# Layer 1's v in two chunks of 1024 columns, all of it by the seven products, with banks of 512 and the token operands from a transposed difference of rows

## The chip, the core and the metric
The kernel runs on one core of a Trainium2 chip. The metric is the device time of one launch in microseconds (us), lower is better. The engines are TensorE (PE, matmuls; PEld are its weight loads), VectorE (DVE), ScalarE (ACT), GpSimdE (POOL) and SyncE (SP), which issues the transfers. Each works through a queue of its own in the order in which the program was scheduled, and waits for semaphores of the others.

## The reference, cut to what matters
Two layers act on 1024 tokens of 1024 channels. Layer 0 is gated recurrence beside windowed attention with one output projection. Layer 1 is a gated MLP whose input projection has three parts of 2048 columns:

```python
h = rms_norm(x, norm_c[j])
z = h @ w_in_c[j]                       # 1024 x 1024 by 1024 x 6144
u, v, g = split_cols(z, (GMLP_WIDTH, GMLP_WIDTH, GMLP_WIDTH))
v = layer_norm(v, ln_v_g[j], ln_v_b[j])
sg = chunked_spatial_gating(v, spatial_w[j], spatial_b[j])
y = u * sg * jax.nn.silu(g)
x = x + y @ w_out_c[j]
```
This case is about v = h @ w_in_c[:, 2048:4096] and the statistics of its layer norm.

## The kernel before
Every float32 operand of a matmul is split into a high and a low part (`hi` by a cast on ACT, `lo` by a subtract on DVE), and `mm3` (lines 145 to 148) multiplies by three matmuls: high by high, high by low, low by high. Larger products are done by Winograd's form of the 2 x 2 block product, seven block products instead of eight, which needs sums and differences of the blocks of both factors. `winograd` (line 739) does so for layer 0's output projection in 14 steps `s`; each step has 48 matmuls of 512 columns, and `operands(s + 1)` is prepared during step s. Its hook `out_a_after` (line 1027) starts layer 1's work: row norms as the token tiles (128 tokens each) come out, and the transposes of tiles 0 to 3 (`norm_c_transpose`) in steps 12 and 13.

Tokens fall into two halves and channels (the contraction) into two halves, so h has the blocks b11, b21 (tokens 0 to 511, channel halves 0 and 1), b12, b22 (tokens 512 to 1023). The token operands t1 = b12 - b11, t2 = b22 - t1, t3 = b22 - b12 and t4 = b21 - t2 serve v, the gate g and u. v is made in two ways:
- columns 0 to 511 (`v_tile`, line 987): plainly, eight token tiles by eight channel blocks, 192 matmuls of 512 columns, with weights from the list of prefetched weights (`weight("v", j)`). Behind each of the first four token tiles PE transposes one of the tiles 4 to 7, and ACT and DVE make its token operands out of the transposed banks (`token_sums`, line 1063); `token_sum_last` makes t4 during tiles 4 to 7.
- columns 512 to 2047 in three chunks of 512 (`v_chunk`, line 1136): seven products, each of 4 token tiles by 4 channel blocks by three matmuls of 256 columns, two tiles sharing a bank. `v_operands` makes the weight operands: `make(i)` one of the seven, its sums where needed, then a cast on ACT and a subtract on DVE.

Results go through `vst` tiles to `vdram`, statistics of 256 columns (`bn_stats`) into `st_all`; behind v the statistics are aggregated and the groups of g and u follow (`group_operands`, `group_gate`), whose first raw weights use the two `raw` buffers.

Order: PE keeps the program's order throughout. The block from `v_tile(0)` to the end of the groups is a `manual_schedule` of ACT, DVE, POOL and SP too: each keeps the program's order inside it, as inside winograd's block ahead of it; where two blocks meet, the scheduler may let the head of the second run ahead of the tail of the first. Buffers: `wpool` has five high and five low weight tiles, `rawpool` two tiles, `big` 16 tiles of 8 KB a partition, PSUM eight banks. The pool `vp` (40 KB a partition) lies where winograd's pool `po` lay, and a tile of it waits until the tiles that lay there were last used.

Of the kernel before, what the change touches and what calls it, by code (L numbers as in the profile page):

```python
# [62 lines left out]
def trunk_kernel(  # L63
# [52 lines left out]
    for j in range(4):  # L116
        add_spec(("v", j), cols_k2(w_in_c, 256 * j, GW))

    wtiles, raws = [], {}
    ahead, last_spec = [0], [index["v", 0] - 1]  # L120

    def fetch_weights(i):

        for j in range(len(raws), min(i, last_spec[0]) + 1):
            raws[j] = rawpool.tile([P, specs[j].shape[1], specs[j].shape[2]], F32, tag="raw", name=f"raw{j}")
            nc.sync.dma_start(out=raws[j], in_=specs[j])

    def load_weights(i, prefetch=True):

        for j in range(len(wtiles), min(i, last_spec[0]) + 1):  # L130
# [850 lines left out]
    st_all = const_c.tile([P, NT, 8, 6], F32, name="st_all")  # L981

    def v_stats(t, g, src):
        for i in range(2):
            nc.vector.bn_stats(out=st_all[:, t, g + i, :], in_=src[:, i * 256:(i + 1) * 256])

    def v_tile(t):
        acc = bank(f"v0_{t}")
        for k in range(8):
            wh, wl = weight("v", k // 2)  # L990
            mm3(acc, h_at(h1h, k, t * P, P), h_at(h1l, k, t * P, P), wh[:, k % 2, :], wl[:, k % 2, :],
                k == 0, k == 7)
# [9 lines left out]
    def norm_c_transpose(t):  # L1002
        for hs, part in ((h1h, "h"), (h1l, "l")):
            for i in range(2):
                if hs[i][t // 4] is None:
                    hs[i][t // 4] = big_tile(F32R, f"g{part}{i}{t // 4}").rearrange("p (k s) -> p k s", k=4)
        return list(norm_transpose(x1_row(t), f"c{t}", h1h, h1l, t))
# [18 lines left out]

    def out_a_after(s, j, m):
# [17 lines left out]
    last_spec[0] = len(specs) - 1  # L1045
    p4.close()
    p5 = ExitStack()
    late["vp"] = p5.enter_context(tc.tile_pool(name="vp", bufs=1, reuse_waits="tile"))


    tsum = [[None] * 2 for _ in range(4)]
    t2_tiles = [late["vp"].tile([P, 2, 4, P], F32, tag=f"vsum{i}", name=f"t2w{i}") for i in range(2)]
    t2_whole = [t2_tiles[i // 2][:, i % 2] for i in range(4)]

    def token_split(i, c, src):
# [3 lines left out]
        hi, lo = [part[:, :, c * P:(c + 1) * P] for part in tsum[i]]  # L1059
        nc.scalar.copy(out=hi, in_=src)  # L1060
        nc.vector.tensor_tensor(out=lo, in0=src, in1=hi.bitcast(F32), op=ALU.subtract)

    def token_sums(c, banks):

        b12, b22 = banks
        b11h, b11l = [part[0][0][:, :, c * P:(c + 1) * P].bitcast(F32) for part in (h1h, h1l)]
        t1, t3 = [late["vp"].tile([P, 4, P], F32, tag="sum", name=f"t{i}w{c}", bufs=4) for i in (1, 3)]
        t2 = t2_whole[c]
        nc.scalar.copy(out=t3, in_=b12)
        nc.vector.tensor_tensor(out=t1, in0=b12, in1=b11h, op=ALU.subtract)  # L1070
        nc.vector.tensor_tensor(out=t1, in0=t1, in1=b11l, op=ALU.subtract)
        nc.vector.tensor_tensor(out=t2, in0=b22, in1=t1, op=ALU.subtract)
        token_split(0, c, t1)
        nc.vector.tensor_tensor(out=t3, in0=b22, in1=t3, op=ALU.subtract)
        token_split(1, c, t2)
        token_split(2, c, t3)

    def token_sum_last(c):

        b21h, b21l = [part[1][0][:, :, c * P:(c + 1) * P].bitcast(F32) for part in (h1h, h1l)]  # L1080
        t2 = t2_whole[c]
        nc.vector.tensor_tensor(out=t2, in0=b21h, in1=t2, op=ALU.subtract)
        nc.vector.tensor_tensor(out=t2, in0=t2, in1=b21l, op=ALU.add)
        token_split(3, c, t2)

    def v_operands(vc):

        raw = []
        for d in range(2):
            for kh in range(2):  # L1090
                pool, tag = (late["vp"], f"raw{kh}") if d else (rawpool, "raw")
                raw.append(pool.tile([P, 4, 256], F32, tag=tag, name=f"rawv{vc}_{d}{kh}"))
                nc.sync.dma_start(out=raw[-1], in_=cols_k4(w_in_c, kh, GW + vc * 512 + d * 256))
        a11, a12, a21, a22 = raw
        sums, ops = [], []

        def make(i):
            if i == 2:
                sums.extend(late["vp"].tile([P, 4, 256], F32, tag=f"vsum{j}", name=f"vs{vc}_{j}") for j in range(2))
                nc.vector.tensor_tensor(out=sums[0], in0=a21, in1=a22, op=ALU.add)  # L1100
                nc.vector.tensor_tensor(out=sums[1], in0=sums[0], in1=a11, op=ALU.subtract)
            elif i == 4:
                nc.vector.tensor_tensor(out=a11, in0=a11, in1=a21, op=ALU.subtract)
            elif i == 5:
                nc.vector.tensor_tensor(out=a12, in0=a12, in1=sums[1], op=ALU.subtract)
            src = [a11, a12, *sums[::-1], a11, a12, a22][i] if i > 1 else raw[i]
            hi = wpool.tile([P, 4, 256], F32R, tag="wh", name=f"whv{vc}_{i}")
            lo = wpool.tile([P, 4, 256], F32R, tag="wl", name=f"wlv{vc}_{i}")
            nc.scalar.copy(out=hi, in_=src)
            nc.vector.tensor_tensor(out=lo, in0=src, in1=hi.bitcast(F32), op=ALU.subtract)  # L1110
            ops.append((hi, lo))

        return ops, make

    manual = tc.manual_schedule(engines={ET.Activation, ET.DVE, ET.Pool, ET.SP})
    manual.__enter__()
    for t in range(4):
        v_tile(t)
        token_sums(t, norm_c_transpose(4 + t))
    for t in range(4, NT):  # L1120
        v_tile(t)
        if t == 4:
            ops, make = v_operands(1)
            make(0)
        token_sum_last(t - 4)
    b11, b21, b22 = [(h1h[i][j], h1l[i][j]) for i, j in ((0, 0), (1, 0), (1, 1))]
    bops = {"b11": b11, "b21": b21, "b22": b22, "t1": tsum[0], "t2": tsum[1], "t3": tsum[2], "t4": tsum[3]}

    plan = [(0, False, "b11"), (1, False, "b21"), (0, True, "t2"), (2, False, "t1"), (0, True, "t3"), (2, True, "b22"),
            (0, True, "t4")]  # L1130
# [317 lines left out]
```

## Time and profile before

| | us |
|---|---|
| median of 3 runs | 1338.87 (1338.86 to 1339.13) |
| profiled execution | 1339.43 |
| its span, first to last instruction | 1337.7 |
| mean granted TensorE clock in it | 0.998 of 2.4 GHz |

The profile is of one execution, and durations are taken from it. 1.73 us of its time lie outside the span. A page gives the busy share of each engine; the trace behind it is asked by views: groups of instructions by line, the timeline of one engine, busy time by stretches, waits, the chain that ended last, transfers. Matmuls are pipelined, so the time of one is longer than its distance to the next; the distance from start to start is what PE pays.

### The profile page before, as it was taken

Reading aid. Unit: us, or ns where it says so; the run is one execution under the profiler, and the core shown is the slowest. Engines: PE = TensorE matmul, PEld = TensorE weight load, DVE = VectorE, ACT = ScalarE, POOL = GpSimd, SP = SyncE. Lnnn points to the kernel's source line nnn. Section 1 sums busy time; section 2 is a strip of 40 time slices with the busy share of each in tenths; the row PEclk is TensorE's granted clock in tenths of the full one; section 3 lists DMA queues with packets and bytes.
Section 4 is the critical chain, followed back from the end, with each engine's and each line's share of the span. In section 5 each row is a group of like instructions: output and inputs, shape, how many; then the busy total and the mean of one; then the engine's idle time right before and its main releaser. Section 6 shows DMA issues by size and latency. Waiting matters only on the chain.

```text
span 1337.7 us, 17905 instructions
## 1 busy us (share of the span) xinstructions
PE 1312.3 (98%) x6775; PEld 1119.6 (84%) x6775; DVE 968.0 (72%) x1594; ACT 690.9 (52%) x1246; POOL 236.3 (18%) x240
## 2 busy tenths in 40 slices
PE   7999999999999999999998999999999999999998
PEld 6988888888878888788887999888888888888887
DVE  6568787877678988987896655585666656579873
ACT  6467777786497776344553223334434444433431
POOL 3345555655323322000000000000000000000000
PEclk9999999999999999999999999999999999999999
DMA  6011111111311106413312332413333233596131
GB/s 226 23 58 49 32 49 32 48 49 32 87 40 56 36 5 231 162 48 142 111 53 90 126 111 80 156 57 111 103 112 110 70 110 103 195 376 231 48 110 63
DMA packets 97170, 131.38 MB, mean 98 GB/s; under 512 B 4907, under 2 KB 68540, under 8 KB 95036
## 3 DMA queue, kind: packets, MB, share of 16 engines
q1 hardware_dynamic: 97084, 130.24, 28.9%
q8 instruction: 53, 0.87, 0.3%
q14 instruction: 33, 0.27, 0.1%
HBM read 105.03 MB, written 25.19 MB: 97 GB/s over the span
## 4 chain that ended last, share of the span: by engine, by line
PE 72%; DVE 13%; ACT 7%; DMA 4%; issue 3%; SPq 0%; POOL 0%; DVEq 0%; ACTq 0%
PE m L146 6%; PE m L148 6%; PE m L147 6%; PE u L147 4%; PE u L148 4%; PE u L146 4%; PE g L146 4%; PE g L147 4%; PE g L148 4%; PE v L146 3%; PE v L147 3%; PE v L148 3%; PE s L1329 2%; PE pq L146 2%; PE pq L148 2%
## 5 line engine op out<-in xcount | busy, mean ns | idle before, releaser
L146 PE MATMUL m<-wh_w,wa 128*128 128x512 f32 x432 | 168.6, 390 | 1.6 <-DVE x L853 1.6
L148 PE MATMUL m<-wh_w,wa 128*128 128x512 f32 x432 | 168.1, 389 | 0.0
L147 PE MATMUL m<-wl_w,wa 128*128 128x512 f32 x432 | 168.1, 389 | 0.0
L146 PEld LDWEIGHTS m<-wh_w,wa 128*128 128x128 f32 x432 | 81.1, 188 | 19.2 <-ACT wa L718 1.8
L148 PEld LDWEIGHTS m<-wh_w,wa 128*128 128x128 f32 x432 | 81.1, 188 | 16.9
L147 PEld LDWEIGHTS m<-wl_w,wa 128*128 128x128 f32 x432 | 81.1, 188 | 16.6
L725 ACT CAST wh_w<-b 128x1024 fp32r<-128x1024 f32 x36 | 37.7, 1047 | 75.4 <-DVE b L820 54.2
L550 DVE CUSTOM_DVE_ANT_0 e<-ps,e,sink_bc 128x256 f32<-128x256 f32 (+1 forms) x128 | 62.0, 520 | 3.1 <-POOL e L525 2.6
L135 DVE TENSOR_TENSOR wl<-raw,wh 128x1024 fp32r<-128x1024 f32 x38 | 50.6, 1337 | 16.4 <-ACT wh L134 16.3
L566 ACT ACTIVATE e<-e,nm 128x256 f32<-128x256 f32 (+1 forms) x128 | 61.4, 481 | 0.0
L853 DVE TENSOR_TENSOR x<-m,x 128x512 f32<-128x512 f32 x56 | 36.6, 685 | 29.5 <-PE m L148 29.5
L1301 ACT ACTIVATE sg<-sg 128x512 f32<-128x512 f32 x24 | 15.2, 632 | 70.4 <-DVE sg L1300 70.4
L574 POOL TENSOR_TENSOR e<-e 128x512 f32<-128x512 f32 x28 | 37.2, 1327 | 80.2 <-ACT e L566 80.2
L146 PE MATMUL pq<-hh,wh 128*128 128x512 f32 x128 | 50.4, 394 | 0.0
L146 PE MATMUL ga<-hh,wh 128*128 128x512 f32 x128 | 50.1, 392 | 0.3 <-ACT z L873 0.3
L146 PE MATMUL gb<-hh,wh 128*128 128x512 f32 x128 | 50.1, 391 | 0.0
L148 PE MATMUL pq<-hh,wl 128*128 128x512 f32 x128 | 50.0, 390 | 0.0
L147 PE MATMUL pq<-hl,wh 128*128 128x512 f32 x128 | 50.0, 390 | 0.0
L148 PE MATMUL gb<-hh,wl 128*128 128x512 f32 x128 | 49.9, 390 | 0.0
L148 PE MATMUL ga<-hh,wl 128*128 128x512 f32 x128 | 49.9, 390 | 0.0
L147 PE MATMUL gb<-hl,wh 128*128 128x512 f32 x128 | 49.9, 390 | 0.0
L147 PE MATMUL ga<-hl,wh 128*128 128x512 f32 x128 | 49.9, 390 | 0.0
(401 smaller groups left out, 4039.2 us busy)
## 6 DMA issues: line engine op xcount, KB each, us to landing
raw<-in_w_in_a_dram SPq DMA_DIRECT2D x34, 512.0 KB, 4.0
b<-in_w_out_a_dram SPq DMA_DIRECT2D x22, 512.0 KB, 3.4
b<-in_w_out_c_dram SPq DMA_DIRECT2D x22, 512.0 KB, 6.0
rawg<-in_w_in_c_dram SPq DMA_DIRECT2D x16, 512.0 KB, 3.6
rawu<-in_w_in_c_dram SPq DMA_DIRECT2D x16, 512.0 KB, 3.5
vg<-vdram SPq DMA_DIRECT2D x8, 1024.0 KB, 6.1
ydram<-ug SPq DMA_DIRECT2D x32, 256.0 KB, 2.4
yg<-ydram SPq DMA_DIRECT2D x8, 1024.0 KB, 8.2
```

The lines of the kernel that those rows point to most:

```text
L135: nc.vector.tensor_tensor(out=lo, in0=raws[j], in1=hi.bitcast(F32), op=ALU.subtract)
L146: nc.tensor.matmul(acc, lhsT=lh, rhs=rh, start=first, stop=False, skip_group_check=shared)
L147: nc.tensor.matmul(acc, lhsT=lh, rhs=rl, start=False, stop=False, skip_group_check=shared)
L148: nc.tensor.matmul(acc, lhsT=ll, rhs=rh, start=False, stop=last, skip_group_check=shared)
L550: nc.vector.tensor_tensor_reduce(out=e[:, h, k0:256], in0=acc[:, j * 256:j * 256 + kw], in1=e[:, h, k0:256], scale=rs[:, 2 * (b % 4) + j:2 ...
L566: nc.scalar.activation(out=e[:, h], in_=e[:, h], func=AF.Exp, bias=st["nm"][:, h:h + 1], accum_out=st["sums"][:, h:h + 1])
L574: nc.gpsimd.tensor_tensor(out=p, in0=p, in1=e[:, :, P:256], op=ALU.add)
L725: nc.scalar.copy(out=hi, in_=src)
L853: nc.vector.tensor_tensor(out=dst, in0=accs[m], in1=dst, op=add)
L1301: nc.scalar.activation(out=c, in_=c, func=AF.Silu)
L1329: nc.tensor.matmul(acc[:, i * P:(i + 1) * P], lhsT=vgs[g][:, half * 4 + i, d * P:(d + 1) * P], rhs=ws_t[:, g, :], start=True, stop=True)
```

## The change
The plain pass over columns 0 to 511 is gone, and with it `v_stats`, `v_tile`, `token_sums`, `token_sum_last` and the v entries of the prefetched weights. v is made in two chunks of 1024 columns by the seven products with 512-column matmuls, one bank for each token tile. `v_weights` replaces `v_operands`: quarters of 512 x 512 as two tiles of 256 rows, a21 loaded twice (once into the tile that becomes the running sum, once for a11 - a21). a11's load is issued in winograd's step 11, its split made in step 13. `token_tile` takes t1's rows as a difference of normalised rows ahead of the transposes and runs behind each token tile of the first product; b12 is no longer made. `token_less` makes t3 = t2 - b11 and t4 = b21 - t2 in products 2 to 5 of chunk 0. Evictions, stores (256 KB each) and statistics (512 columns) go by token tile. `vp` has 12 `vst` tiles of 2 KB and 4 `braw` tiles of 4 KB. `st_all` has four sets of statistics a token tile instead of eight. The first group's operands are made in products 4 to 6 of chunk 1. The removed functions are printed above; of the diff the core:

```diff
-    for j in range(4):
-        add_spec(("v", j), cols_k2(w_in_c, 256 * j, GW))
...
-    st_all = const_c.tile([P, NT, 8, 6], F32, name="st_all")
+    st_all = const_c.tile([P, NT, 4, 6], F32, name="st_all")
...
+    def v_weights(vc):
+        nh = 4 + 2 * vc
+        q = {"a11": raw_quarter(w_in_c, 0, nh, f"va{vc}_")}
+        ops = []
+        def fetch(*names):
+            for name in names:
+                if name == "sum":
+                    whole = big_tile(F32, f"vx{vc}").rearrange("p (j k s) -> p j k s", j=2, k=2)
+                    q["sum"] = load_quarter(lambda j: whole[:, j], w_in_c, 0, nh + 1)
+                else:
+                    d, kh = int(name[1]) - 1, int(name[2]) - 1
+                    q[name] = load_quarter(
+                        lambda j: late["vp"].tile([P, 2, 512], F32, tag="braw", name=f"v{vc}{name}_{j}", bufs=4),
+                        w_in_c, kh * 512, nh + d)
+        def make(i):
+            name, *of = (("a11",), ("a12",), ("sum", "sum", "a22", ALU.add), ("sum", "sum", "a11", ALU.subtract),
+                         ("sum", "a12", "sum", ALU.subtract), ("a21", "a11", "a21", ALU.subtract), ("a22",))[i]
+            parts = []
+            for j in range(2):
+                if of:
+                    nc.vector.tensor_tensor(out=q[name][j], in0=q[of[0]][j], in1=q[of[1]][j], op=of[2])
+                parts.append(split_b(q[name][j], f"v{vc}_{i}_{j}"))
+            ops.append(parts)
+        return ops, make, fetch
...
+        if s == 11 and (j, m) == (0, 0):
+            late["v"] = v_weights(0)
...
+        if s == 13 and (j, m) == (0, 0):
+            late["v"][1](0)
...
+    def token_parts(dst, c, src):
+        hi, lo = [part[:, :, c * P:(c + 1) * P] for part in dst]
+        nc.scalar.copy(out=hi, in_=src)
+        nc.vector.tensor_tensor(out=lo, in0=src, in1=hi.bitcast(F32), op=ALU.subtract)
...
+    def token_tile(c):
+        row, other = x1_row(4 + c), x1_row(c)
+        diff = token_rows(f"diff{c}").rearrange("p k s -> p (k s)")
+        nc.vector.tensor_tensor(out=diff, in0=row[:, :512], in1=other[:, :512], op=ALU.subtract)
+        t1, b22 = [bank(f"ptd{c}_{i}").rearrange("p (k s) -> p k s", k=4) for i in range(2)]
+        for dst, src in ((t1, diff), (b22, row[:, 512:])):
+            for k in range(4):
+                nc.tensor.transpose(dst[:, k, :], src[:, k * P:(k + 1) * P], ident)
+        for hs, part in ((h1h, "h"), (h1l, "l")):
+            if hs[1][1] is None:
+                hs[1][1] = big_tile(F32R, f"g{part}11").rearrange("p (k s) -> p k s", k=4)
+        t1_rows = token_rows(f"t1w{c}")
+        nc.scalar.copy(out=t1_rows, in_=t1)
         token_split(0, c, t1)
+        nc.vector.tensor_tensor(out=t2_whole[:, c], in0=b22, in1=t1_rows, op=ALU.subtract)
+        token_parts((h1h[1][1], h1l[1][1]), c, b22)
+        token_split(1, c, t2_whole[:, c])
+    def token_less(i, c):
+        h, l = [part[i - 2][0][:, :, c * P:(c + 1) * P].bitcast(F32) for part in (h1h, h1l)]
+        t2 = t2_whole[:, c]
+        if i == 2:
+            dst = token_rows(f"t3w{c}")
+            nc.vector.tensor_tensor(out=dst, in0=t2, in1=h, op=ALU.subtract)
+            nc.vector.tensor_tensor(out=dst, in0=dst, in1=l, op=ALU.subtract)
+        else:
+            dst = t2
+            nc.vector.tensor_tensor(out=dst, in0=h, in1=t2, op=ALU.subtract)
+            nc.vector.tensor_tensor(out=dst, in0=dst, in1=l, op=ALU.add)
+        token_split(i, c, dst)
...
+        products = [(0, False, "b11", (0, 0), 0), (1, False, "b21", (0, 0), 1), (1, False, "t1", (1, 1), 0),
+                    (0, True, "t2", (0, 1), 0), (1, True, "b22", (0, 1), 1), (0, True, "t3", (1, 1), 1),
+                    (0, True, "t4", (1, 0), 2)]
+        sets, vs = {}, {}
+        def stats(d, th, m):
+            nc.vector.bn_stats(out=st_all[:, 4 * th + m, 2 * vc + d, :], in_=vs[d, th, m])
+        for i, (bank_set, adds, bop, (d, th), act) in enumerate(products):
+            run(steps.get((i, -1), []))
+            if not adds:
+                sets[bank_set] = [None] * 4
+            bh, bl = operand_b(bop)
             for m in range(4):
+                if not adds:
+                    sets[bank_set][m] = bank(f"v{vc}_{i}_{m}")
+                acc = sets[bank_set][m]
+                tok = slice(m * P, (m + 1) * P)
                 for k in range(4):
+                    ah, al = ops[i][k // 2]
+                    mm3(acc, bh[:, k, tok], bl[:, k, tok], ah[:, k % 2, :], al[:, k % 2, :], not adds and k == 0,
+                        k == 3, shared=True)
+                if act == 1:
+                    dst = vs[d, th, m]
+                    nc.vector.tensor_tensor(out=dst, in0=acc, in1=dst, op=ALU.add)
                 else:
+                    dst = vs[d, th, m] = vp.tile([P, 512], F32, tag="vst", name=f"v{vc}_{d}{th}{m}", bufs=12)
+                    nc.scalar.copy(out=dst, in_=acc)
+                if act:
+                    nc.sync.dma_start(
+                        out=vdram[4 * vc + 2 * d:4 * vc + 2 * d + 2, :, 4 * th + m, :].rearrange("g p c -> p g c"),
+                        in_=dst.rearrange("p (g c) -> p g c", g=2))
+                if i in (1, 6):
+                    stats(d, th, m)
+                if i in (5, 6):
+                    stats(*((0, 1) if i == 5 else (1, 1)), m)
+                run(steps.get((i, m), []))
...
+    v_ops = late["v"]
+    v_ops[2]("a12", "a22", "sum")
...
+    for vc in range(2):
+        ops, make, fetch = v_ops
+        steps = {(i, -1): [(make, i + 1)] for i in range(6)}
+        steps[4, -1].insert(0, (fetch, "a21"))
+        if vc == 0:
+            for c in range(4):
+                steps[0, c] = [(token_tile, c)]
+            for i, m, kind, c in ((2, 0, 2, 0), (2, 1, 2, 1), (2, 2, 2, 2), (3, 0, 2, 3), (3, 1, 3, 0), (3, 2, 3, 1),
+                                  (4, 1, 3, 2), (5, 0, 3, 3)):
+                steps[i, m] = [(token_less, kind, c)]
+            def next_weights():
+                late["v"] = v_weights(1)
+                late["v"][2]("a12", "sum")
+            steps[5, -1].append((next_weights,))
+            steps[6, -1] = [(lambda: late["v"][2]("a22"),), (lambda: late["v"][1](0),)]
+        else:
+            steps[4, -1].append((first_group,))
+            steps[4, 3] = [(first_group_steps, 0)]
+            steps[5, 2] = [(first_group_steps, 1)]
+            steps[6, -1] = [(first_group_steps, 2)]
+            steps[6, 1] = [(first_group_steps, 3)]
+            steps[6, 3] = [(first_group_steps, 5, 6)]
         v_chunk(vc, ops, steps)
+        v_ops = late["v"]
```

## Rows read from the trace of the kernel before

**Rows 1.** The page's busy times: engine, busy us (share of span) x instructions.
```profile
PE 1312.3 (98%) x6775; PEld 1119.6 (84%) x6775; DVE 968.0 (72%) x1594; ACT 690.9 (52%) x1246; POOL 236.3 (18%) x240
```
**Rows 2.** Stretches: length, busy PE PEld DVE ACT POOL (x instructions), clock, DMA, GB/s.
```profile
667.97:715.07 47.10, 47.10 (x226) 39.35 (x225) 37.10 (x62) 21.65 (x38) 1.10 (x2) 1.00 0.28 93
715.07:762.22 47.15, 42.57 (x338) 41.97 (x336) 32.45 (x46) 15.50 (x20) 0.00 (x0) 0.96 0.27 90
762.22:802.54 40.32, 40.32 (x339) 40.32 (x337) 22.30 (x33) 11.62 (x15) 0.00 (x0) 1.00 0.31 105
802.54:842.86 40.32, 40.32 (x339) 40.32 (x337) 21.71 (x37) 10.96 (x17) 0.00 (x0) 1.00 0.21 79
```
**Rows 3.** PE's timeline, first chunk: start, us, line, operands [idle before, releaser].
```profile
722.01 0.38 PE L146 MATMUL v<-whv,gh 128*128 128x256 f32 x1 [1.03 <-ACT whv L1109]
...
731.83 0.38 PE L146 MATMUL v<-whv,t1h 128*128 128x256 f32 x1 [2.67 <-ACT vst L1153]
...
739.18 0.28 PE L146 MATMUL v<-whv,t0h 128*128 128x256 f32 x1
```
**Rows 4.** Stretches as in rows 2, around these waits; the clock is third from the end.
```profile
720.00:724.00 4.00, 2.09 (x16) 1.69 (x15) 3.06 (x4) 1.57 (x2) 0.00 (x0) 1.00 0.00 0
...
732.00:736.00 4.00, 4.00 (x23) 4.00 (x24) 2.83 (x4) 2.26 (x3) 0.00 (x0) 0.60 0.00 0
```
**Rows 5.** The chain that ended last, 673 to 732: start, us, what.
```profile
701.30 5.29 DMA rawv<-in_w_in_c_dram
...
723.13 1.23 DVE vs L1100
```
**Rows 6.** PE's timeline: matmuls of 512 columns, and transposes between two of them.
```profile
654.19 0.39 PE L148 MATMUL m<-wh_w,wa 128*128 128x512 f32 x1
654.42 1.03 PE L204 MATMUL ptc<-ident,x 128*128 128x128 f32 x8
...
655.52 0.40 PE L147 MATMUL m<-wl_w,wa 128*128 128x512 f32 x1
...
701.24 0.39 PE L148 MATMUL v<-wh,gl 128*128 128x512 f32 x1
...
701.92 0.39 PE L148 MATMUL v<-wh,gl 128*128 128x512 f32 x1
```
**Rows 7.** DVE's timeline: a sum of weights, its low part, the next sum.
```profile
729.00 1.22 DVE L1103 TENSOR_TENSOR rawv<-rawv,rawv 128x1024 f32<-128x1024 f32 x1
731.33 1.23 DVE L1110 TENSOR_TENSOR wlv<-rawv,whv 128x1024 fp32r<-128x1024 f32 x1 [1.11 <-ACT whv L1109]
732.47 1.22 DVE L1105 TENSOR_TENSOR rawv<-rawv,vs 128x1024 f32<-128x1024 f32 x1
```
**Rows 8.** DVE's timeline: t4 of one token tile, then statistics.
```profile
708.84 0.69 DVE L1082 TENSOR_TENSOR t2w<-gh,t2w 128x512 f32<-128x512 f32 x1
...
711.55 0.76 DVE L985 BATCH_NORM_STATS2 st_all<-v 128x6 f32<-128x256 f32 x2
```
**Rows 9.** DVE's timeline: the last norm; two evictions and four statistics.
```profile
672.56 1.28 DVE L189 SCALAR_TENSOR_TENSOR x<-x,nrsc,gain_c 128x1024 f32<-128x1024 f32 x1 [1.25 <-DMA x1dram<-x]
...
736.00 1.28 DVE L1155 TENSOR_TENSOR vst<-v,vst 128x512 f32<-128x512 f32 x2
737.19 1.39 DVE L1160 BATCH_NORM_STATS2 st_all<-vst 128x6 f32<-128x256 f32 x4
```
**Rows 10.** ACT's timeline: casts of transposed banks; the fourth v weight's cast.
```profile
655.05 1.07 ACT L209 CAST gh<-ptc 128x512 fp32r<-128x512 f32 x2 [2.16 <-PE ptc L204]
...
666.86 1.05 ACT L134 CAST wh<-raw 128x1024 fp32r<-128x1024 f32 x1 [2.10 <-issue]
```
**Rows 11.** Transfers by line: issues, KB each, median us to landing.
```profile
raw<-in_w_in_c_dram SPq DMA_DIRECT2D x4, 512.0 KB, 3.7
```
**Rows 12.** Timelines of DVE and PE behind v: a raw weight's last read; the wait.
```profile
844.35 0.67 DVE L1189 TENSOR_TENSOR wlg<-rawg,whg 128x512 fp32r<-128x512 f32 x1
...
851.10 0.69 DVE L1181 TENSOR_TENSOR s0u<-rawu,rawu 128x512 f32<-128x512 f32 x1 [1.91 <-DMA rawu<-in_w_in_c_dram]
...
855.34 0.50 PE L146 MATMUL g<-t2h,whg 128*128 128x512 f32 x1 [1.41 <-ACT sg L1295]
```

More of the change, by code (lines that the diff above doesn't have):

```diff
@@ L128, in load_weights @@
     def load_weights(i, prefetch=True):
-        for j in range(len(wtiles), min(i, last_spec[0]) + 1):
+        for j in range(len(wtiles), min(i, len(specs) - 1) + 1):
             fetch_weights(j)
@@ L1006, in norm_c_transpose @@
                     hs[i][t // 4] = big_tile(F32R, f"g{part}{i}{t // 4}").rearrange("p (k s) -> p k s", k=4)
[L1007 removed]
+        list(norm_transpose(x1_row(t), f"c{t}", h1h, h1l, t))
     def x1_done(t, nh, dst):
@@ L1078, in token_sum_last @@
[L1078 to L1127, printed above, removed]
@@ L1144, in v_chunk @@
                 for k in range(4):
-                    tok = slice(m * P, (m + 1) * P)
-                    mm3(acc, bh[:, k, tok], bl[:, k, tok], ah[:, k, :], al[:, k, :], not adds and k == 0 and m % 2 == 0, k == 3,
-                        shared=True)
-            first = i in (0, 2, 3)
-            q = {0: 0, 1: 0, 2: 1, 3: 3, 4: 3, 5: 1, 6: 2}[i]
-            for h in range(2):
-                dst = vs[q][:, h * 512:(h + 1) * 512]
-                if first or i == 6:
-                    nc.scalar.copy(out=dst, in_=sets[j][h])
-                else:
-                    nc.vector.tensor_tensor(out=dst, in0=sets[j][h], in1=dst, op=ALU.add)
@@ L1156, in v_chunk @@
-            if not first:
-                d, th = divmod(q, 2)
-                v = vs[q].rearrange("p (t c) -> p t c", t=4)
-                for m in range(4):
-                    nc.vector.bn_stats(out=st_all[:, 4 * th + m, 2 * vc + d, :], in_=v[:, m, :])
-                nc.sync.dma_start(out=vdram[2 * vc + d, :, 4 * th:4 * th + 4, :], in_=v)
-            run(steps.get(i, []))
+                    ah, al = ops[i][k // 2]
+                    mm3(acc, bh[:, k, tok], bl[:, k, tok], ah[:, k % 2, :], al[:, k % 2, :], not adds and k == 0,
+                        k == 3, shared=True)
@@ L1165, in group_operands, with first_group, first_group_steps @@
+    following = []
+    def first_group():
+        following.extend(group_operands(*order[0]))
+    def first_group_steps(*which):
+        for i in which:
+            run(following[1][i])
     def group_operands(kind, g):
@@ L1177, in add_up @@
         def add_up(i):
-            sums.append(late["vp"].tile([P, 4, P], F32, tag="sum", name=f"s{i}{kind}{g}", bufs=4))
+            tag, bufs = ("vst", 12) if late["vp"] is vp else ("sum", 4)
+            sums.append(late["vp"].tile([P, 4, P], F32, tag=tag, name=f"s{i}{kind}{g}", bufs=bufs))
             p, q, op = ((a21, a22, ALU.add), (sums[0], a11, ALU.subtract), (a11, a21, ALU.subtract),
```

77 lines of the change are left out of this document (15 added, 62 removed).

## The prediction

> **What bounds the kernel now.** I read the page's busy shares first: TensorE (PE) is busy 98% of the span [rows 1], so only its matmul time and its few gaps can be won, unless another engine is made the bound. Next the table of stretches: layer 1's v runs from 667.97 to 842.86 us, 174.89 us in four parts: the first 512 columns 47.10, then three chunks of 47.15, 40.32 and 40.32 us [rows 2]. The two equal chunks are PE without a gap; the 47.15 is the same work with 6.83 us too much. The timeline of PE shows where: waits of 1.03 and 2.67 us at 722 and 731.8 [rows 3], and behind the second a stretch whose mean granted clock is 0.60 [rows 4]. The first 48 matmuls after it, up to 739.18, last 7.35 us where 48 x 0.12 = 5.76 are due, so the lowered clock cost 1.6 us. The chain of waits runs there through a weight load and VectorE (DVE) [rows 5]: at this transition PE is bound by work on vectors, not by matmuls. That is what to look for in the change as well.
>
> **PE's part.** A 256-column matmul takes 40.32 / 336 = 0.12 us [rows 2]. Three 512-column ones take 701.92 - 701.24 = 0.68, so 0.2267 each; eight transposes put 655.52 - 654.19 - 2 x 0.2267 = 0.88 between two matmuls [rows 6]. At 2.4 GHz 512 columns are 213.3 ns and 256 are 106.7, so either kind pays some 13 ns more per matmul, and halving the number halves that. Removed: 192 x 0.2267 + 1008 x 0.12 = 43.5 + 121.0 = 164.5 us. Added: 2 chunks x 7 products x 48 = 672 matmuls, 152.3 us. Both have 32 transposes in four lots (3.6 with rounding). Without any wait, v would end at 667.97 + 152.3 + 3.6 = 823.9, which is 19.0 us early: 12.2 of matmuls and 6.8 of old stall.
>
> The Trainium skill ("TensorE: Matmul & The Clock Gate", section "Back-to-back issue gap") gives N/2.4 + 2.5 ns per warm matmul. By it the same counts would save 151.5 - 145.0 = 6.5 us instead of 12.2, and the forecast below would come out at about 1340; both pitches are in the trace and each is 11 ns above that rule, so the measurement decides and I give the rule no chance of its own.
>
> **What the vector engines must do meanwhile.** The four engines beside PE keep the program's order. Prices, all start to start:
> - Half an operand (`make`, i = 2 to 5): subtract 1024 on DVE, cast on ScalarE (ACT), subtract on DVE. DVE waits inside for ACT: 729.00 to 731.33 to 732.47, 3.5 us [rows 7]. The new loop does whole halves one after the other, with nothing between to fill the wait: 7.0 us an operand. Operands without a sum (i = 0, 1, 6) cost 2.3.
> - One `token_less`: two dependent subtracts, ACT's cast, a subtract: 708.84 to 711.55, 2.7 us [rows 8].
> - A 512 eviction by DVE 0.6, as two take 737.19 - 736.00 [rows 9] (0.7 if the next instruction reads it). The 512-wide statistics have no row; four of 256 last 1.39 us [rows 9], 0.35 each. Bounds 0.35 (no dearer than 256) and 0.75 (two of 256); I take 0.6, as for other 512-wide ones. An eviction with statistics is then 1.3, four are 5.2.
> - One `token_tile`: transposes to ACT's first read of a bank 0.6 (654.42 to 655.05) and on ACT a copy and a cast of 0.5 each [rows 6, 10], then on DVE four operations of 0.6, one waiting for ACT, and the next tile's difference (0.6 to 0.7). The difference feeds PE's next transposes, so the tiles form a ring of 0.6 + 1.0 + 4 x 0.6 + 0.7 and some 0.5 of hand-overs, 5.2 us; PE has 12 matmuls and 8 transposes for it, 3.6. Each further tile stalls PE 1.6. If DVE found no wait in the ring, its 3.2 us would hide and the stall be 0.
>
> **Walking DVE's order through chunk 0.** DVE ends the norms of tile 7 at 672.56 + 1.28 = 673.8 [rows 9]. The second half of `make(1)` waits for a weight buffer that the last winograd product frees, as the fourth v weight does now at 666.86 [rows 10], so the first difference comes between 669 and 672, when PE wants it at 670.7: stall 0 to 1.4, and the first tile's DVE work starts at 673.9 either way. Four tiles end on DVE at 692.1; PE leaves product 0 at 688.5 instead of 682.5 (stall 6.0). Then, in program order:
> - make(2) to 699.1, product 1's evictions with statistics to 704.3. PE's product 2 needs their banks: product 1 ends at 699.4, the first bank is out at 699.8 (stall 0.4).
> - make(3) to 711.3, three token_less to 719.4, make(4) to 726.4. PE's product 4 starts at 721.6 and needs both halves: stalls 3.3 in its first 12 matmuls, ends 735.8.
> - three token_less to 734.5, make(5) to 741.5. Product 5 stalls 4.2, ends 750.9.
> - evictions and the last token_less are done well before product 6 needs them; product 6 ends 761.8.
> Chunk 1 has no token work: DVE needs 7.0 us an operand in 10.9 us a product, and I find no wait in it. 761.8 + 7 x 10.88 = 837.9. With the difference late or statistics at 0.75 it is 838.6; if the norm tail fills DVE's waits 836.7. I take 838.1: **4.8 us early**, stalls being 14.2 where they were 6.8.
>
> Costed at nothing: a11's two loads and `make(0)`, moved into winograd's steps 11 and 13, and the loads of a12, a22 and a21 behind it: they take on SP, ACT and DVE the places of the four v loads and splits of now, ahead of the norms' stores, with 4 MB for 2 MB (the late case is a rival); behind `make(0)` winograd's first eviction comes up to 1.2 us later, but the norms' end hangs on the last one. ACT's evictions (ACT is busy 11 of 40 us in a chunk [rows 2]; where it waits for DVE, they wait in that order and are done a product before their bank is wanted); the reload of a21 (issued when make(4) has read a12 at about 724, needed at 734.5; a lone 512 KB load lands in 3.7 us [rows 11]; later than that it would add its lateness); stores per 256 KB instead of 512 KB, behind which only loads with over 5 us to spare queue on SP.
>
> **Behind v.** The gate stage waits 1.41 us at 855.34, since ACT's copy stands behind a sum that needs the next raw weights, which land for 851.10 after the last read of the old ones at 844.35 [rows 12], 1.5 us after v's end. In the new order that read stands behind two statistics and two more subtracts, 3.2 us after v's end: up to 1.7 later. But the queue ahead is lighter (a store of 256 KB in place of 512 KB, the first raw load long gone), so the load may land up to 0.6 sooner. I take 0.3.
>
> **Sum.** 4.8 - 0.3 = 4.5 us off the span: 1337.7 to 1333.2, the profiled execution 1339.4 to 1334.9, and the median shown, 0.56 below the profiled one, 1338.87 to 1334.4.
>
> **Rivals.**
> - The clock falls on the path. Product 5's waits are 1.0 to 1.1 each; around the wait of 1.03 us the granted clock stayed 1.00, after the one of 2.67 it was 0.60 [rows 3, 4]. But four in 5.8 us may count as one. A fall in products 0 to 4 is absorbed by the waits that follow; one in product 5 or at the gate stage costs 1.6 each. With one and the upper bounds 1336.5, with two and all of them 1340. For it: 4.2 us of wait within 5.8. Against: no single gap is as long as 2.67.
>   The Trainium skill (same page, "Part 1: The HAM clock gate") says that the clock is halved by default and that activity releases it; the 0.60 after the 2.67 us wait agrees.
> - Slower: `make(1)` heads the new block, so ACT and DVE reach the first difference only behind a12's landing. Its buffers lie where winograd's pool lay. If they overlie the weight tiles, free once winograd's last operands are made, it lands long before. If they overlie the norms' gain, read until 673.8 [rows 9], the load starts then, lands 3.7 later [rows 11] and is split by 680.9; PE waits 10.9 us for the first difference and v ends at 847.4: 4.5 + 0.3 slower, 1343.7, or 1345 with the clock. It decides from a landing after about 669. Against: if a pool lies in the order of first use, the old one begins with the weight tiles, and so does the new.
> - The vector work hides: if order on DVE lets PE run through, 19.0 - 0.3 gives 1320; half of the chunk's stalls gone 1327. Against: the ring and the 7.0 us are rows, and at this very transition DVE already binds.
>
> **How the numbers follow.** Forecast 0.50 (1332.5 to 1336), clock and upper bounds 0.27 (1336 to 1341), late a12 0.15, hidden 0.08. This kernel's measurement can tell about 0.2%, 2.7 us, from no change: faster is below 1336.2, 0.50 + 0.08 = 0.58; same 0.27; slower 0.15. The range takes the forecast with its bounds and the clock: 1331 to 1341.
>
> **What would show it.** In the PE timeline: waits of about 1.6 us at three lots of transposes, on DVE's difference; about 1 us each at the start of products 4 and 5 of chunk 0, on a cast or a subtract of weights; chunk 1 in 76 us without a gap; v 170 us long. DVE near 100% busy or waiting for ACT from 674 to 741. Wrong if chunk 1 stalls, if the first transposes wait beyond 673 (late a12), or if the gate stage's wait exceeds 3 us.

## The result, and the profile after

The changed kernel takes 1346.40 us (median, 1345.17 to 1347.21), the kernel before 1338.86 on the same chip (1338.04 to 1339.13): ratio 1.0052, 95% interval 1.0040 to 1.0064. It is 7.5 us **slower**; 1334.4 was forecast, with a range that ended at 1341. The profiled execution took 1346.60, its span 1344.9 against 1337.7, 7.2 longer. Cut at v's ends: 0.3 shorter ahead of v (it begins at 667.69), 8.0 longer in v (182.88 us against the 174.89 of [rows 2]), 0.5 shorter behind it.

The page's busy times after (as in [rows 1]):
```profile
PE 1307.4 (97%) x6247; PEld 1091.4 (81%) x6247; DVE 974.2 (72%) x1571; ACT 691.7 (51%) x1245; POOL 236.5 (18%) x240
```
PE has 528 matmuls fewer and is 5 us less busy, in a span that is 7 us longer: what was lost are waits and a lower clock, not work. The table of stretches of the changed kernel, by product: products 0 to 6 of chunk 0, then chunk 1 (columns as in [rows 2]):
```profile
667.69:698.20 30.51, 17.54 (x81) 13.88 (x80) 17.17 (x24) 12.48 (x23) 1.10 (x2) 0.83 0.29 104
698.20:710.80 12.60, 12.60 (x52) 10.24 (x51) 8.66 (x11) 4.19 (x6) 0.00 (x0) 0.86 0.01 1
710.80:721.68 10.88, 10.88 (x50) 9.01 (x49) 8.46 (x11) 2.59 (x3) 0.00 (x0) 1.00 0.28 96
721.68:732.56 10.88, 10.88 (x50) 9.01 (x48) 7.54 (x12) 4.38 (x7) 0.00 (x0) 1.00 0.04 5
732.56:747.33 14.77, 11.90 (x50) 8.67 (x48) 10.27 (x14) 5.90 (x9) 0.00 (x0) 1.00 0.21 68
747.33:763.53 16.20, 14.48 (x49) 10.62 (x49) 13.60 (x18) 4.52 (x6) 0.00 (x0) 0.79 0.47 141
763.53:774.41 10.88, 10.88 (x50) 9.01 (x48) 9.30 (x14) 3.54 (x5) 0.00 (x0) 1.00 1.07 358
774.41:850.57 76.16, 76.16 (x338) 63.06 (x336) 46.19 (x56) 23.12 (x32) 0.00 (x0) 1.00 0.29 95
```
The prediction's walk gave 20.5, 10.9, 11.3, 10.9, 14.2, 15.1, 10.9 and 76.2, together 170.0. Of the 12.9 us that are too many, 10.0 are in product 0, 1.7 in product 1 and 1.7 in products 4 and 5 (product 2 gives 0.4 back). Two columns tell two causes apart: where PE's busy time is short of the length, PE waited (product 0 by 13.0 us); where the clock is below 1, the granted clock had fallen for a part of the stretch (products 0, 1 and 5). PE's timeline of the changed kernel has the places; its second to fourth lines are half-clock matmuls behind the first wait, the lines after them the waits at the last two token tiles, inside product 4 and at the head of product 5:
```profile
679.68 1.09 PE L1093 MATMUL ptd<-ident,diff 128*128 128x128 f32 x4 [9.11 <-DVE diff L1089]
...
681.84 0.63 PE L145 MATMUL v<-wl_v,gh 128*128 128x512 f32 x1
682.27 0.63 PE L146 MATMUL v<-wh_v,gl 128*128 128x512 f32 x1
...
684.40 0.52 PE L145 MATMUL v<-wl_v,gh 128*128 128x512 f32 x1
...
691.60 0.66 PE L1093 MATMUL ptd<-ident,diff 128*128 128x128 f32 x4 [1.90 <-DVE diff L1089]
...
697.38 0.63 PE L1093 MATMUL ptd<-ident,diff 128*128 128x128 f32 x4 [1.93 <-DVE diff L1089]
...
735.68 0.50 PE L144 MATMUL v<-wh_v,gh 128*128 128x512 f32 x1 [0.84 <-ACT wh_v L723]
...
747.33 0.50 PE L144 MATMUL v<-wh_v,t2h 128*128 128x512 f32 x1 [0.80 <-ACT wh_v L723]
```
The wait of 9.11 us for the first difference is more than the whole loss, and nothing like it stood in the forecast but in the rival "late a12". The queues at that place show why. SP's timeline of the changed kernel (issues; `va` is a11, `vx` the sum's tile, `v0a` a12 and a22):
```profile
637.98 3.90 SPq L731 DMA_DIRECT2D va<-in_w_in_c_dram  x2
641.94 0.97 SPq L731 DMA_DIRECT2D vx<-in_w_in_c_dram  x2
...
667.09 3.16 SPq L994 DMA_DIRECT2D x1dram<-x  x2
670.29 2.43 SPq L731 DMA_DIRECT2D v0a<-in_w_in_c_dram  x4
```
ACT's timeline there:
```profile
675.24 1.04 ACT L723 CAST wh_v<-v0a 128x1024 fp32r<-128x1024 f32 x1 [4.10 <-DMA v0a<-in_w_in_c_dram]
676.62 1.04 ACT L723 CAST wh_v<-v0a 128x1024 fp32r<-128x1024 f32 x1 [0.34 <-DMA v0a<-in_w_in_c_dram]
```
DVE's timeline there:
```profile
673.06 1.28 DVE L187 SCALAR_TENSOR_TENSOR x<-x,nrsc,gain_c 128x1024 f32<-128x1024 f32 x1 [1.68 <-DMA x1dram<-x]
676.32 1.23 DVE L724 TENSOR_TENSOR wl_v<-v0a,wh_v 128x1024 fp32r<-128x1024 f32 x1 [1.97 <-ACT wh_v L723]
677.70 1.22 DVE L724 TENSOR_TENSOR wl_v<-v0a,wh_v 128x1024 fp32r<-128x1024 f32 x1 [0.16 <-ACT wh_v L723]
678.85 0.68 DVE L1089 TENSOR_TENSOR diff<-x,x 128x512 f32<-128x512 f32 x1
```
a12's load goes out at 670.29, behind the last of the norms' stores, and lands at 675.2. `make(1)` heads the block, so ACT and DVE stand at it until 678.9, and only then comes the first difference, of rows whose later norm (tile 4's, begun at 663.55) had ended at 664.8.

### The profile page after: what moved, and what is told of

Its sections match the earlier page's. It is cut to its first block, busy times and chain, and to the rows that moved or that the text cites. A ratio compares the mean times of both kernels' runs of the same rounds, so it can differ in the third digit from the quotient of the medians.

```text
span 1344.9 us, 16867 instructions
## 1 busy us (share of the span) xinstructions
PE 1307.4 (97%) x6247; PEld 1091.4 (81%) x6247; DVE 974.2 (72%) x1571; ACT 691.7 (51%) x1245; POOL 236.5 (18%) x240
## 4 chain that ended last, share of the span: by engine, by line
PE 70%; DVE 16%; ACT 8%; issue 3%; DMA 2%; SPq 0%; POOL 0%; DVEq 0%; ACTq 0%
PE m L144 6%; PE m L146 6%; PE m L145 6%; PE u L145 4%; PE u L146 4%; PE u L144 4%; PE g L144 4%; PE g L145 4%; PE g L146 4%; PE v L145 3%; PE v L144 3%; PE v L146 3%; PE s L1352 2%; DVE e L548 2%; PE gb L146 1%
## 5 line engine op out<-in xcount | busy, mean ns | idle before, releaser
L133 DVE TENSOR_TENSOR wl<-raw,wh 128x1024 fp32r<-128x1024 f32 x34 | 45.7, 1350 | 16.1 <-ACT wh L132 15.8
L724 DVE TENSOR_TENSOR wl_w<-b,wh_w 128x1024 fp32r<-128x1024 f32 x36 | 46.2, 1283 | 5.3 <-ACT wh_w L723 5.1
```

The lines of the kernel that those rows point to most:

```text
L133: nc.vector.tensor_tensor(out=lo, in0=raws[j], in1=hi.bitcast(F32), op=ALU.subtract)
```

## The experiments

Theory after this reading: three separate losses, (1) the first difference, late by a12's load and by its own place in DVE's order, (2) the ring of the token tiles, (3) the stalls of products 4 and 5, where DVE waits inside each half of an operand; and, behind all three, the falls of the clock. The rival for each is that the place where PE was seen to wait is not the cause, and that the wait turns up elsewhere. All times are medians against the kernel before on the same chip (1339.3 to 1339.5 there); the length of v comes from the trace of each. A trace is of one execution, which can lie off the median (1328.17 in the run with a12, norms and sums, 2.5 above it), so the two columns need not move by the same amount:

| kernel | v, us | time, us | ratio to before (95%) |
|---|---|---|---|
| before | 174.89 | 1338.86 | |
| changed | 182.88 | 1346.40 | 1.0052 (1.0040 to 1.0064) |
| a12 early | 177.15 | 1342.88 | 1.0025 (1.0016 to 1.0035) |
| differences in the norms | 175.58 | 1339.58 | 1.0001 (0.9992 to 1.0010) |
| both | 172.26 | 1335.13 | 0.9963 (0.9949 to 0.9978) |
| turns in a token tile | 178.16 | 1343.91 | 1.0036 (1.0023 to 1.0048) |
| both sums first | 171.76 | 1337.49 | 0.9984 (0.9975 to 0.9994) |
| a12, norms, sums | 161.33 | 1325.71 | 0.9898 (0.9883 to 0.9914) |
| the same and turns | 159.30 | 1326.04 | 0.9902 (0.9887 to 0.9917) |
| a12, norms, sums; quiet | 161.26 | 1323.15 | 0.9881 (0.9867 to 0.9894) |
| the same and turns; quiet | 159.26 | 1321.49 | 0.9869 (0.9855 to 0.9882) |
| before; quiet | 173.64 | 1336.92 | 0.9984 (0.9975 to 0.9993) |

**a12 early.** The big tile, whose load the trace shows at 641.94, goes to a12, and the sum takes the tiles that are loaded late:
```diff
-                if name == "sum":
+                if name == "a12":
                     whole = big_tile(F32, f"vx{vc}").rearrange("p (j k s) -> p j k s", j=2, k=2)
-                    q["sum"] = load_quarter(lambda j: whole[:, j], w_in_c, 0, nh + 1)
+                    q["a12"] = load_quarter(lambda j: whole[:, j], w_in_c, 512, nh)
                 else:
-                    d, kh = int(name[1]) - 1, int(name[2]) - 1
+                    d, kh = (1, 0) if name == "sum" else (int(name[1]) - 1, int(name[2]) - 1)
```


> Edit: the quarter a12 takes the big tile that the running sum had, and the sum takes the vp tiles of a12; so a12's load no longer waits for the pool vp and can be issued with a11's, near 642 us, ahead of the last norm stores. Nothing else. Theory A (late load): in the changed kernel the first transposes wait 9.11 us because DVE and ACT stand behind a12, issued at 670.3 behind the last store. With the load early the first difference follows the last norm, which ends at 674.3, so the wait falls from 9.1 to about 3.8 and the rest of chunk 0 moves forward as a whole: 5.3 us less, 7 if the clock stays up there: 1339.5 to 1341.1. Theory B (vector chain alone): the loss is in the ring of token tiles and in the 7.0 us operands, and the wait only moves to the next place: under 2 us less, above 1344.4.

Measured 1342.88, between the two: 3.5 us back of 7.5 (4.0 when each is set against the kernel before on its own chip). The wait fell from 9.11 to 5.46 only. DVE's timeline of this run shows what is next in line:
```profile
673.74 1.28 DVE L187 SCALAR_TENSOR_TENSOR x<-x,nrsc,gain_c 128x1024 f32<-128x1024 f32 x1 [1.66 <-DMA x1dram<-x]
675.06 0.69 DVE L1089 TENSOR_TENSOR diff<-x,x 128x512 f32<-128x512 f32 x1
```
a12's splits are out of the way, and the first difference (tiles 0 and 4) still stands behind the norm of tile 7, which waits for a store of its row. So the late load was one half of the wait and the place of the difference the other.

**Differences in the norms, without and with the early load.** Each difference becomes the last step of the norm of tiles 4 to 7, in place over the rows of tiles 0 to 3:
```diff
                           lambda: norm_mul(xt, xt, rs[0], late["gain_c"])])
+            if t >= 4:
+                norms[-1].append(lambda: nc.vector.tensor_tensor(
+                    out=x1_row(t - 4)[:, :512], in0=xt[:, :512], in1=x1_row(t - 4)[:, :512], op=ALU.subtract))
...
-             out_a_after, lambda: [norms_step(0) for _ in range(2)])
+             out_a_after, lambda: [norms_step(0) for _ in range(3)])
...
-        row, other = x1_row(4 + c), x1_row(c)
-        diff = token_rows(f"diff{c}").rearrange("p k s -> p (k s)")
-        nc.vector.tensor_tensor(out=diff, in0=row[:, :512], in1=other[:, :512], op=ALU.subtract)
+        row, diff = x1_row(4 + c), x1_row(c)[:, :512]
```


> Edit: only the differences are moved into the norms (the early-load run and the norms run together had 1335.1); a12's load stays behind the last norm store. Asks which of the two made the wait of 9.1 us ahead of the first transposes. Theory A (both stand in the way, one behind the other): PE gets the first transposes at about 671 to 674, runs on through the eight banks, and then waits for the first token tile's vector work, which stands behind a12's splits on DVE (they end at 678.9 in the changed kernel, where the norms end at 674.3): so product 0 ends some 3 to 4 us later than in the run with both, and the time is 1337.5 to 1339.5, which is 7 to 9 below the changed kernel. Theory B (the place of the differences alone, the late load hides in the banks): 1335 to 1336, the same as with both. Theory C (the late load alone): the wait stays near 9 and the time above 1344.

Measured 1339.58, 6.8 below the changed kernel and 4.5 above the run with both, just above theory A's range. PE no longer waits for a difference but for the first token tile's vector work, behind a12's splits. PE's timeline of this run:
```profile
680.71 1.02 PE L1094 MATMUL ptd<-ident,x 128*128 128x128 f32 x4 [2.55 <-DVE t0l L1077]
```


> Edit: a12 early as in e1_early_a12, and the four differences of rows are made in winograd's block as a last step of each norm of tiles 4 to 7, in place over the rows of tiles 0 to 3. Then no transposes wait for DVE's order. Theory A with the ring as the second part: product 0 lasts 14.4 us instead of 30.5 and the clock's two falls around it go; from product 1 on the chain of 7.0 us operands binds as before: product 5 ends near 743.5, or 745.3 with the clock's fall there, where it is 763.5 now: 18 to 20 us less, 1326.4 to 1328.4. If the waits in product 0 are due to something else (banks, the load itself) 1335 or more.

Measured 1335.13, some 7 us above the range, and by the time the rival's answer (1335 or more). The trace gives each its part. The wait ahead of the first transposes is gone (product 0 takes 17.98 us, not 30.51), but 14.4 was expected: waits of 1.18, 0.52 and 1.26 us for banks that DVE still reads are left. And of the 12.5 us won, 3.2 are given back in products 1 and 2 (a wait of 2.93 us for an eviction by DVE stands at the head of product 2), products 4 and 5 still take 13.6 and 16.1, and the clock fell for 17 matmuls. What made the first wait is settled; I had expected too much of it, since PE, once early, only meets the rest of DVE's order sooner.

**Both sums first.** In `make` the two subtracts come ahead of the two splits, so ACT casts one half while DVE subtracts the other:
```diff
             for j in range(2):
                 if of:
                     nc.vector.tensor_tensor(out=q[name][j], in0=q[of[0]][j], in1=q[of[1]][j], op=of[2])
+            for j in range(2):
                 parts.append(split_b(q[name][j], f"v{vc}_{i}_{j}"))
```


> Edit: make(i) does both sums first and then both splits, so that DVE does not wait for the cast of the half that it has just made; 4.9 us an operand instead of 7.0. Nothing else. Theory A and the walk of the prediction: the stalls of products 4 and 5 of chunk 0 (3.9 and 5.3 us in the changed kernel, the clock's fall within them) go, since make(4) would end near 730 and make(5) near 743, each ahead of its product: 9.2 us less, 1337.2; the first wait stays at 9.1. Rival: DVE is bound by the amount of its work in products 1 to 4 and not by its waits; then at most the 2.1 us of one operand are won before the next product binds: about 1344.

Measured 1337.49, as expected. The stretches of this run (product 0; 1; 2 and 3; 4 and 5):
```profile
669.81:700.01 30.20, 19.17 (x82) 15.37 (x80) 16.68 (x24) 12.56 (x23) 1.10 (x2) 0.77 0.29 105
700.01:711.01 11.00, 11.00 (x52) 9.10 (x50) 9.27 (x12) 4.19 (x6) 0.00 (x0) 1.00 0.06 21
711.01:732.77 21.76, 21.76 (x98) 18.02 (x96) 19.45 (x24) 8.50 (x12) 0.00 (x0) 1.00 0.26 85
732.77:754.53 21.76, 21.76 (x98) 18.02 (x96) 18.60 (x25) 8.15 (x12) 0.00 (x0) 1.00 0.29 89
```
Products 4 and 5 run through: 21.76 for 30.97; an operand with its sum now takes DVE 4.7 us (739.65 to 744.32). One added line takes 11.1 us off v, the late load 5.7.

**Turns in a token tile.** In the changed kernel ACT's cast of b22 waits until DVE has read the same bank for t2. ACT's timeline of the changed kernel, third tile:
```profile
692.78 0.59 ACT L1073 CAST t0h<-ptd 128x512 fp32r<-128x512 f32 x1
694.73 0.59 ACT L1073 CAST gh<-ptd 128x512 fp32r<-128x512 f32 x1 [1.36 <-DVE t2w L1100]
```
and DVE's, which then waits for that cast:
```profile
693.40 0.69 DVE L1074 TENSOR_TENSOR t0l<-ptd,t0h 128x512 fp32r<-128x512 f32 x1 [1.86 <-ACT t0h L1073]
694.01 0.68 DVE L1100 TENSOR_TENSOR t2w<-ptd,t1w 128x512 f32<-128x512 f32 x1
695.35 0.69 DVE L1074 TENSOR_TENSOR gl<-ptd,gh 128x512 fp32r<-128x512 f32 x1 [0.66 <-ACT gh L1073]
```
The edit puts all three reads of ACT first; `lows` holds back the subtracts:
```diff
         nc.scalar.copy(out=t1_rows, in_=t1)
-        token_split(0, c, t1)
+        lows = []
+        token_split(0, c, t1, lows)
+        token_parts((h1h[1][1], h1l[1][1]), c, b22, lows)
+        lows[0]()
         nc.vector.tensor_tensor(out=t2_whole[:, c], in0=b22, in1=t1_rows, op=ALU.subtract)
-        token_parts((h1h[1][1], h1l[1][1]), c, b22)
+        lows[1]()
         token_split(1, c, t2_whole[:, c])
```


> Edit: only the order within a token tile: the cast of b22 ahead of t2's subtract, so that ACT's three reads of the two banks are not interleaved with DVE's. Theory A (the ring of 5.7 instead of 5.2 us is ACT waiting 1.35 us for DVE's read of the same bank, and DVE then 0.65 for that cast): the waits of 1.9 at tiles 2 and 3 fall to 1.2 or less, product 0 ends 2 us earlier, and since DVE is the bound up to product 5 the gain is kept: 1343.7 to 1344.6 (before the edit 1346.4). Theory B (the ring is DVE's own work, and the wait is only taken elsewhere): 1346 to 1346.8.

Measured 1343.91, theory A: the waits at tiles 2 and 3 fell from 1.9 to 1.34 and 1.37 us (1.2 or less was expected), product 0 from 30.51 to 28.31, of which 0.5 is a shorter first wait (8.59). DVE's work on the four tiles takes 18.21 us (684.19 to 702.40), 2.2 less than in the changed kernel (20.45). ACT's timeline of this run has the cast without a wait:
```profile
693.94 0.59 ACT L1073 CAST t0h<-ptd 128x512 fp32r<-128x512 f32 x1
694.42 0.60 ACT L1073 CAST gh<-ptd 128x512 fp32r<-128x512 f32 x1
```
v got 4.7 us shorter in the traces; the 2.5 beyond product 0 are mostly clock (11 half-speed matmuls instead of 21).

**All together.** The early load, the norms and the sums in one kernel:

> Edit: a12 early, differences in the norms, and both sums ahead of both splits. All three causes gone, v is PE's 672 matmuls and 32 transposes without a wait, 155.9 us instead of 182.9: 27 us less, 1319.4, up to 1321 with a longer wait at the gate stage. If a fourth cause exists (DVE's amount of work, stores, the weight buffers), it shows as a wait in chunk 0 and the time stays above 1323.

Measured 1325.71: 13.7 below the kernel before, 20.7 below the changed one, but above 1323. The edits add: v lost 10.6 by the first two, 11.1 by the sums, and 21.6 by all three. What is left are mainly banks of the token tiles that come free late, in PE's timeline of this run:
```profile
682.22 0.47 PE L144 MATMUL v<-wh_v,gh 128*128 128x512 f32 x1 [1.25 <-DVE gl L1078]
686.14 0.63 PE L1095 MATMUL ptd<-ident,x 128*128 128x128 f32 x4 [0.48 <-DVE gl L1078]
688.03 0.50 PE L144 MATMUL v<-wh_v,gh 128*128 128x512 f32 x1 [1.26 <-DVE t0l L1078]
```
With the new turns added:

> Edit: the run with all three (early load, differences in the norms, both sums first; 1325.7) with the new order within a token tile added. Theory A (the fourth cause, its waits of 1.26, 0.48, 1.26 and 0.59 in products 0 and 1, is the two engines taking turns at b22's bank): DVE's ring falls from 3.93 us a tile to 2.5 to 3.3, the first wait to about 0.4 (DVE begins the first tile behind the last norm either way) and the others to nothing: 1322.0 to 1323.2. Theory B (banks are late for another reason): 1325 to 1326.

Measured 1326.04, theory B by the time and theory A by the trace: v is 2.0 us shorter (159.30). Both can't be the end of it, so I looked ahead of v.

**A wait ahead of v that is in every kernel.** In the runs so far v begins at about 667.6 or about 670. The difference arises at 555 us, in winograd's step 3, where a sum of 2.35 us on DVE stands ahead of the evictions that PE waits for. The stretch 550 to 560 us in the changed kernel:
```profile
550.00:560.00 10.00, 8.57 (x38) 6.77 (x37) 10.00 (x11) 3.89 (x4) 0.00 (x0) 1.00 0.24 72
```
and in the run with everything and the new turns:
```profile
550.00:560.00 10.00, 7.78 (x28) 5.97 (x27) 10.00 (x12) 3.44 (x4) 0.00 (x0) 0.83 0.19 60
```
Ten matmuls fewer in the same time. PE waits there 1.43 us in the one and 2.22 in the other, because a weight load landed 0.7 us later (ACT's cast of that weight, released by the load, begins at 536.02 in the one and at 536.75 in the other), and behind the longer wait the clock fell. Three runs have that sum behind the evictions ("quiet"); in their traces PE has no wait in this stretch:
```diff
-            for args in early.get(s, []):
+            for args in early.get(s, []) if s != 3 else []:
                 sums_a(*args)
...
                 after(s, j, m)
+            if s == 3:
+                sums_a(*early[3][0])
             ops = nxt
```


> Edit: the run with the early load, the differences in the norms and both sums first (1325.7), with one sum of winograd's step 3 (2.35 us on DVE) moved behind that step's evictions. Asks whether the wait that stands there in every trace, 110 us ahead of v, hides what the edits to v do: PE waits 1.3 to 2.5 us for an eviction behind that sum, by how late a weight load lands in this execution, and behind waits of 1.80 and more the granted clock fell (some ten matmuls at half speed, 2.3 us), behind those of 1.30 to 1.45 it did not. Theory A (that wait and fall are a spread laid over all kernels): both are gone from the trace, v begins at 666 to 667, and the time falls by 1.4 to 4: 1321.7 to 1324.3. Theory B (the load only makes PE wait elsewhere): 1325 to 1326.5.

Measured 1323.15, 2.6 less than without the moved sum.

> Edit: the same with the new order within a token tile as well (1326.0 without the moved sum). The new order shortened v from 161.3 to 159.3 in the traces but the medians did not show it. Theory A (the fall ahead of v hid it): 1.3 to 2.5 below the run beside this one, 1320 to 1322.5. Theory B (the order is worth nothing, and the profiled execution without it was a long one): within 0.7 of the run beside this one.

Measured 1321.49, 1.7 below the run beside it: the turns are worth nearly what the traces said (2.0), and the medians show it once the spread ahead of v is gone.

> Edit: the kernel before with the same sum moved and nothing else. Theory A (the wait of 1.45 is on the path whatever follows, and some executions add a fall of the clock): 1.4 to 3 below the kernel before, 1336.5 to 1338. Theory B: 1339 to 1340.

Measured 1336.92, 2.4 below the kernel before. All three fell as theory A had it. The fastest kernel is thus 1.3% below the kernel before, and 15.4 us below the kernel before with the same quiet step: that much the change to v and the order of its vector work are worth together. Not all of it need be the change: in the quiet kernel before, v takes 173.64 us where its parts without a stall would take 47.10 + 3 x 40.32 = 168.06 [rows 2], and its vector work was left as it is. Up to 5.6 of the 15.4 us may be order that the kernel before could have as well, which was not tried. The stretches of v in the fastest kernel (product 0; 1; 2 to 6; chunk 1):
```profile
666.29:683.28 16.99, 15.04 (x81) 12.25 (x79) 13.66 (x20) 9.48 (x18) 1.17 (x3) 1.00 0.52 186
683.28:694.30 11.02, 11.02 (x48) 9.12 (x49) 10.04 (x13) 5.30 (x8) 0.00 (x0) 1.00 0.01 2
694.30:749.39 55.09, 54.74 (x242) 44.98 (x240) 49.18 (x65) 20.72 (x29) 0.00 (x0) 1.00 0.43 139
749.39:825.55 76.16, 76.16 (x338) 63.08 (x336) 46.36 (x57) 23.17 (x32) 0.00 (x0) 1.00 0.30 103
```
159.26 us against the 155.9 that the prediction gave for PE's work alone.

## Why the prediction was wrong

- **PE's part** held: chunk 1 takes 76.16 for 76.2 without a gap. By the Trainium skill's pitch (the section named in the prediction, which gives it for an isolated matmul) it would be an estimated 336 x 0.2158 = 72.5; the trace decides.
- **Prices of the vector work** held. DVE's timeline of the changed kernel: the start of its work on the token tiles and what follows that work, statistics of 512 columns and what follows them, the head of a `token_less`, the next, an operand with its sum and what follows it, and what follows `make(5)`:
```profile
681.91 0.69 DVE L1074 TENSOR_TENSOR t0l<-ptd,t0h 128x512 fp32r<-128x512 f32 x1 [2.38 <-ACT t0h L1073]
...
702.36 1.22 DVE L1033 TENSOR_TENSOR vx<-vx,v0a 128x1024 f32<-128x1024 f32 x1
...
710.03 0.69 DVE L1132 BATCH_NORM_STATS2 st_all<-v 128x6 f32<-128x512 f32 x1
710.64 0.67 DVE L1150 TENSOR_TENSOR v<-v,v 128x512 f32<-128x512 f32 x1
...
721.62 0.69 DVE L1110 TENSOR_TENSOR t3w<-t2w,gh 128x512 f32<-128x512 f32 x1
...
724.33 0.68 DVE L1110 TENSOR_TENSOR t3w<-t2w,gh 128x512 f32<-128x512 f32 x1
...
729.74 1.22 DVE L1033 TENSOR_TENSOR vx<-v0a,vx 128x1024 f32<-128x1024 f32 x1
...
736.80 0.69 DVE L1110 TENSOR_TENSOR t3w<-t2w,gh 128x512 f32<-128x512 f32 x1
...
751.98 1.28 DVE L1150 TENSOR_TENSOR v<-v,v 128x512 f32<-128x512 f32 x2
```
  A `token_less` takes 2.71 us for 2.7, an operand 7.06 for 7.0. The statistics, whose 0.6 was taken between two bounds and not from a row, last 0.69 and take 0.61 from start to start, which is what DVE pays. From the end of the token tiles to the end of `make(5)` the walk has 49.4 us (692.1 to 741.5) and DVE took 49.62. So what DVE lost lies ahead of that: its work on the token tiles began at 681.91 instead of 673.9, 8.0 late, and took 20.45 us instead of 18.2.
- **The ring** was mis-sized: 691.60 to 697.38 is 5.78 us a tile, not 5.2. I counted one wait of DVE for ACT in it; there are two, the second (0.66) because ACT's cast of b22 comes behind DVE's read of the same bank. [rows 10] show ACT's two casts 0.5 apart; I took that for a price and not for one order of reads. The Trainium skill ("PSUM — Partial Sum Buffer", section "PSUM bank collisions raise a hardware error") says that the back end's scheduler puts a dependency between two instructions of different engines that touch one bank in the same 32 partitions, reads with reads too. The wait of 1.36 us agrees: the two instructions share the transposed bank and nothing else. So does its absence with the turns changed.
- **The failed step** is the sentence that put a12's load "ahead of the norms' stores" at no cost, and with it the first difference "between 669 and 672". The load went out at 670.29, the difference at 678.85, and the first wait was 9.11 us where 0 to 1.4 was forecast. I had found the mechanism as the rival "late a12", with 10.9 us and 1343.7 to 1345, and gave it 0.15 because I asked only which memory the tiles lie on. The load went out at 670.29, before the gain's last read at 673.06 ended, so that memory is not what held it. The tiles that were loaded late are those of the pool opened behind winograd's block; the big tile, later in the same call, was loaded at 641.94. In SP's queue a12's load stands behind the last store, which waited for DVE's eviction of tile 7's row; it went out 0.04 us behind that store's issue (667.09 + 3.16 = 670.25), and in the nine other runs of the changed kernel the first load into that pool followed the last store by 0.04 or 0.05 as well. So its place in the queue is what held it there; why it got that place, and whether its memory would have been free earlier, was not separated. And the rival was only half of it: without the late load the difference still stood behind the last norm, 5.46 us late.
- **Stalls of products 4 and 5**: 3.9 and 5.3 us over 10.88, where 3.3 and 4.2 were forecast; the fall of the clock in product 5, some 1.9 us, is more than what it is too long.
- **The clock** fell three times in chunk 0, for 21 matmuls of 0.43 instead of 0.23, some 4.2 us. I expected falls ahead of product 5 to be absorbed, and for product 1's 1.7 us the trace agrees: from 702.36 to 751.98 DVE waits for PE nowhere, and PE's waits in product 4 are for DVE and ACT. No run tried it by itself.
- **Behind v** the gate stage waits 1.05 us, not 1.7 (1.41 before [rows 12]). The last read of the old raw weights came at 853.79, 3.2 us after v's end as forecast, but the load behind it landed 3.9 us after its issue (854.50 to 858.41) and not 6.0 (845.05 to 851.10 before). That the lighter queue of SP made it faster, the smaller of the two effects that I weighed, is argued and not tried.

## What to carry to other kernels

When a change opens a new block of work, find for each engine the last instruction of the old block and the first of the new one, and ask of every load when its issue can go out: a load at the head of a block, in tiles of a pool opened there, can come behind the last stores of the old block, and everything on ACT and DVE that stands behind its split comes late too. Work whose inputs are ready early (a difference of rows) belongs into the block in which they become ready. Where two engines hand halves to each other, issue the first step of both halves before the second of either: 11 us of v here for one added line.

## What the runs showed of the hardware

- At the lower granted clock a 512-column matmul takes 0.427 us (six from 681.84 to 684.40 take 2.56), which is 512 columns at 1.2 GHz with nothing added; at full clock it is 0.227 for 0.213. The 13 ns that the prediction found per matmul are not there at half clock. The Trainium skill ("TensorE: Matmul & The Clock Gate", "Part 1: The HAM clock gate") also has the surcharge at full clock alone, but as 2.5 ns; the rows decide for 13 here.
- At the same place in nine traces PE waited 1.30, 1.43, 1.43, 1.43 and 1.45 us with a granted clock of 1.00 in the stretch around it, and 1.80, 1.88, 2.22 and 2.46 us with 0.83 or 0.84. The length of a wait alone does not decide, though: in the changed kernel the wait of 1.90 us at 691.60 was followed by matmuls at full speed, the one of 1.93 at 697.38 by seven at half speed. Several short waits close together are as unclear: 1.2, 0.5 and 1.3 us in product 0 left the clock alone in the run with a12, norms and sums and were followed by 8 half-speed matmuls in the same run with the quiet step.
